# Where in a group of filling products the attention values are placed: two numbers in the rules that deal filling out

## The chip, the core and the metric

The kernel runs on one core of one Trainium2 chip. The metric is the device time of one execution in microseconds (us), as the median of several runs. A core has a matrix engine (PE, with weight loads shown as PEld), a vector engine (DVE), a scalar engine (ACT), a general engine (POOL) and a queue engine (SP) that issues most DMAs. Each engine works through its own list in order; semaphores hold an instruction until what it needs is done. PE writes only to PSUM, which has eight banks, and DVE and ACT read the banks out.

## The reference

One layer over 1024 tokens of width 1024 is computed in f32. The part that matters here is the mixer at its start, and above all the chunked attention:

```python
hn = rmsnorm(h, norm_mix_g[i])
z = hn @ w_in[i]
u = z[..., :POOL_W]                              # 512 columns: pooling mixer
q, k, v = jnp.split(z[..., POOL_W:], 3, axis=-1) # 8 heads of 64
a = pool_mixer(u, pool_w[i], pool_b[i], pool_scale[i])
# chunks of 64 queries, each with its own chunk and 8 earlier ones
s = jnp.einsum('bqhd,bkhd->bhqk', qb, kb).astype(jnp.float32) * scale + bias
pr = jax.nn.softmax(s, axis=-1).astype(vb.dtype)
o = jnp.einsum('bhqk,bkhd->bqhd', pr, vb)
h = h + jnp.concatenate([a, o], axis=-1) @ w_out[i]
```

After it come a gated MLP with a causal convolution, a gated per-layer embedding and a last norm. The change does not touch them.

## The kernel before

Every f32 product is made of three matmuls of rounded parts: high by high, high by low, low by high (`mm3`, lines 117 to 119). A step in `split` makes the two parts, the high one on ACT (line 122) and the low one on DVE (line 123).

The attention stage goes through 28 units. A unit `u` is a pair of heads `c` and one tile of 128 queries (the first unit of each pair of heads takes two tiles), so seven units make a pair of heads. Unit `u` puts on PE, in this order:

1. the transposes of the probabilities of unit `u - 1` (line 406), which ACT and DVE then copy out of banks 2, 3, 6 and 7 as high and low parts (`probs_out`, lines 424 and 426);
2. the scores of unit `u` (line 383) in banks 4 to 7, on which DVE and ACT then do the softmax: the least value (lines 351 or 355), the exponential (line 363), the reciprocal (line 365) and the scaling (line 361 on DVE, line 359 on ACT);
3. filling: products of the projections still to come, which keep PE at work while the softmax of unit `u` runs;
4. if unit `u - 1` ended a pair of query tiles, its attention values (`values(u - 1)`, lines 448 and 449): the probabilities of 256 queries times `V`, for both heads, in one bank. ACT and DVE then add the two halves of the result into `o32` (lines 451 and 454).

The filling is one long generator. It goes through 24 groups; a group is eight products of three matmuls (512 columns each) into bank 0 or bank 1 in turn, and the four groups of the second half of `V` are made of matmuls of 256 columns. After the last product of a group, DVE copies it out (line 263 for queries and keys, line 556 for the pooling columns, lines 254 and 255 for `V`); queries and keys are then split (lines 292 to 296), and weights of later groups are split when their turn comes (lines 469 and 472). `at[0]` holds how far the open group has come: 0.68 for each product, so 5.44 is the end of a group (5.76 for a group of `V`).

The attention values are put into the bank of the group before the open one. So they have to wait until DVE has copied that group out, and the group after the open one has to wait until lines 451 and 454 have read the values out of its bank. Both distances depend on where in the open group the values stand.

How much filling a unit takes is set by `credit`: each unit adds `ROOM[u % 7]`, each product takes 1. In `values`, more products are taken, at 0.5 each, while the open group has come less far than a bound. ACT and DVE instructions are collected with a due time (`push`) and put out sorted by it (`flush`): each at the unit's end, so their order on ACT and DVE follows the step of the filling at which they came up.

After unit 28, what is left of the filling is done, while ACT and DVE split the output weights and the first half of the attention result (`out_weights`, `cat_o`); then the output projection starts.

Of the kernel before, what the change touches and what calls it, by code (L numbers as in the profile page):

```python
# [73 lines left out]
NU = len(UNITS)  # L74
# [8 lines left out]
def trunk(tc, xT, pT, vecs, w_qk0, w_in, w_v, bias, counts, pool_w, w_out, w_up, w_down,  # L83
# [4 lines left out]
    with tc.tile_pool(name="sb", bufs=1) as sb, \  # L88
# [179 lines left out]
        def push(t, *fns):  # L268

            for n, fn in enumerate(fns):  # L270
                pending.append((t + 0.8 * n, len(pending), fn))

        def flush():
            todo = sorted(pending, key=lambda p: p[:2])
            pending.clear()
            owed.clear()
            for _, _, fn in todo:
                fn()
# [21 lines left out]
        def run_later(n):  # L300
            for fn in later[:n]:
                fn()
            del later[:n]
# [30 lines left out]
        def load_bias(h):  # L334
            b = biasb[h % 3]
            sp.dma_start(b, bias[h])

            def turned():
                act.activation(b, b, AF.Copy, scale=-1.0)
                pool.memset(b[0:64, 576:640], BIG)  # L340
                pool.memset(b[64:128, 0:64], BIG)
            return turned

        def softmax(todo, valued):

            for i, (x, b, ps, S, s_) in enumerate(todo):
                z = 2 * i / len(todo)

                def least(b=b, ps=ps, S=S, s_=s_):
                    if len(ps.shape) == 3:  # L350
                        dve.tensor_tensor_reduce(  # L351
                            S.rearrange("p (a b) -> p a b", a=2), ps,
                            b.rearrange("p (a b) -> p a b", a=2), 1.0, BIG, ALU.add, ALU.min, s_[:, 0:1])
                    else:
                        dve.tensor_tensor_reduce(S, ps, b, 1.0, BIG, ALU.add, ALU.min, s_[:, 0:1])

                def scaled(x=x, S=S, s_=s_):
                    if x:
                        act.activation(S, S, AF.Copy, scale=s_[:, 2:3])
                    else:  # L360
                        dve.tensor_scalar(S, S, s_[:, 2:3], None, ALU.mult)  # L361
                push(1.0 + 0.8 * z, least)
                push(1.9 + 0.85 * z, lambda S=S, s_=s_: act.activation(  # L363
                    S, S, AF.Exp, bias=s_[:, 0:1], scale=-1.0, accum_out=s_[:, 1:2]))
                push(max(2.95 + 0.01 * z, 1.91 + 0.85 * z) if valued else 2.95 + 0.55 * z, lambda s_=s_: dve.reciprocal(s_[:, 2:3], s_[:, 1:2]))
                push(3.9 + 0.1 * z if x else 3.0 + (0.01 if valued else 0.55) * z, scaled)
# [26 lines left out]
        def probs_t(u):  # L393

            c, ts = UNITS[u]
            total = key_tiles(u)

            def place(x, m):
                n = 2 * m + x
                return (2, HD * n) if n < 8 else (6, 384 + HD * (n - 8))  # L400

            for x in range(2):
                for m in range(total):
                    bank, col = place(x, m)
                    for y in range(2):
                        pe.transpose(PS[:, bank + y, col:col + HD], Sb[x][halves[y], m * P:(m + 1) * P],  # L406
                                     ident[halves[y], halves[y]], tile_position=(HD * y, 0))
            todo, m = [], 0
            for t in ts:
                nk = min(t + 1, BANDT)  # L410
                i0 = max(0, t - 4) - (t // 2 * 2 - 4)
                for a, b in ((0, min(nk, 4)), (4, nk)):
                    if b > a:
                        bank, col = place(0, m + a)
                        todo.append((t % 2 * P, i0 + a, i0 + b, bank, PS[:, bank:bank + 2, col:col + 2 * HD * (b - a)]))
                m += nk
            return todo

        def probs_out(todo, valued):
            for q, a, b, bank, ps in todo:  # L420
                src = ps.rearrange("p a (n q) -> p n a q", q=HD)
                hi, lo = [pt[:, a:b, :, q:q + P].rearrange("p k x (a q) -> p (k x) a q", a=2) for pt in PT]
                far = bank > 3
                push(3.5 if far else 0.0, lambda hi=hi, src=src: act.activation(hi, src, AF.Copy))
                push((3.55 if valued else 4.4) if far else 2.5 if valued else 3.7,
                     lambda lo=lo, src=src, hi=hi: dve.tensor_tensor(lo, src, rv(hi), ALU.subtract))  # L426

        credit, turns, valued = 0.0, [], [False]

        def values(u):  # L430
            nonlocal credit
            c_, ts = UNITS[u]
            w = ts[-1] // 2
            if ts[-1] % 2 == 0:
                return
            while c_ >= 2 and len(v_ready) < 2 * w + 2 or u < NU - 1 and at[0] < 1.6:
                next(fill)
                credit -= 0.5
                now[0] += STEP
            flush()  # L440
            ks = list(range(max(0, 2 * w - 4), 2 * w + 2))
            bank = (bankn[0] + 1) % 2 if u < NU - 1 else 5
            Os = [PS[:, bank, 256 * j:256 * j + 256] for j in range(2)]
            for j in range(2):
                O = Os[j]
                for n_, k in enumerate(ks):
                    idx = k - (2 * w - 4)
                    pe.matmul(O, V[:, k, 2 * c_ + j], PT[0][:, idx, j], start=n_ == 0, stop=False)  # L448
                    pe.matmul(O, V[:, k, 2 * c_ + j], PT[1][:, idx, j], start=False, stop=n_ == len(ks) - 1)  # L449
            for j in range(2):  # L450
                act.activation(otmp[halves[j]], Os[j][halves[1 - j]], AF.Copy)  # L451
            for j in range(2):
                a = halves[j]
                dve.tensor_tensor(o32[a, c_, w * 256:(w + 1) * 256], Os[j][a], otmp[a], ALU.add)
# [3 lines left out]
        at = [0]  # L458
# [183 lines left out]
        qk_ready, v_ready = [], []  # L642
        fill = rest()

        def lay_due(u):

            for c, x, h in list(qk_ready):
                if u >= (c - 1) * PER + (0 if x else PER - 1 if h else 2):
                    qk_ready.remove((c, x, h))
                    push(max(4.8, now[0] + 0.4), *lay(c, x, h))  # L650
# [4 lines left out]
        def unit(u):  # L655

            nonlocal credit
            now[0] = 0.0
            if u < NU:
                c, ts = UNITS[u]  # L660
                for h in range(2 if ts[-1] > 3 else 1):
                    while not all((c, x, h) in laid for x in range(2)):
                        next(fill)
                        lay_due(u - 1)
                        flush()
            valued[0] = u > 0 and UNITS[u - 1][1][-1] % 2 == 1
            if u:
                probs_out(probs_t(u - 1), valued[0])
            if u < NU:
                softmax(scores(u), valued[0])  # L670
                if u % PER == PER - 1:
                    for h in (2 * c + 3, 2 * c + 4):
                        if h < N_HEADS:
                            push(3.0, lambda h=h: turns.append(load_bias(h)))
                lay_due(u)
                credit += ROOM[u % PER]
                now[0] = 1.25
                while credit >= 1:
                    now[0] += STEP
                    credit -= 1  # L680
                    if next(fill, True) is False:
                        break
                    lay_due(u)
            else:
                for _ in range(DRAIN):
                    now[0] += STEP
                    next(fill)
            flush()
            if u:
                values(u - 1)  # L690
            if turns and (u % PER == PER - 1 or u % PER == 1):
                turns.pop(0)()
            run_later(LATER)
# [4 lines left out]
        with tc.manual_schedule(engines={mybir.EngineType.Activation, mybir.EngineType.DVE}):  # L698
            for u in range(NU + 1):
                unit(u)  # L700
                if u == NU - PER + 2:
                    sp.dma_start(pw, pool_w)
# [750 lines left out]
```

## Time and profile before

| what | value |
| --- | --- |
| median of 3 runs | 1129.33 us (1129.02 to 1129.41) |
| profiled execution | 1130.02 us |
| its span, first to last instruction | 1128.3 us |
| mean granted PE clock | 0.998 |
| PE busy | 1115.4 us, 99% of the span |
| DVE busy | 855.7 us, 76% |
| ACT busy | 586.3 us, 52% |

The span is followed in microseconds from its start. The units of the attention stage lie between about 54 and 266 us. In a row of the timeline the first number is the start, the second the duration, then come engine, line, operation, tiles and shape; a bracket at the end gives how long the engine was idle before, and what ended that. Matmuls overlap: one of 512 columns is shown with about 0.39 us, though the next starts 0.23 us later. So a wait of PE is read from start to start, and an idle time in a bracket is what is left of it after the modelled end of the matmul before.

### The profile page before, as it was taken

To read this page: it belongs to the slowest core of one execution; us is meant where nothing else is said; L and a number is where in the kernel's file an instruction comes from. 1 tells how busy PE (TensorE), PEld (TensorE's weight loads), DVE (VectorE), ACT (ScalarE), POOL (GpSimd) and SP (SyncE) were. 2 spreads that over 40 slices of the span, in tenths; PEclk is the share of its full clock that TensorE was granted. 3 is DMA by queue.
4 is the path that set the end of the run, shared out by engine and by line. 5 is a ranking of instruction groups with operands and counts; after the bars stand their busy time and mean duration, and the time that the engine had idled before them with its cause. 6 is when DMAs were issued, how large, how long until landed. Compare 5 with 4: busy or idle time off the path is not lost.

```text
span 1128.3 us, 16160 instructions
## 1 busy us (share of the span) xinstructions
PE 1115.4 (99%) x5914; PEld 934.0 (83%) x5914; DVE 855.7 (76%) x1456; ACT 586.3 (52%) x1020; POOL 166.3 (15%) x212
## 2 busy tenths in 40 slices
PE   9999999999999999999999999999999999999997
PEld 7988898888888888888888887888888888888887
DVE  7566766677768879877787777787877889986845
ACT  8376766665664644444443444344444444674634
POOL 0011001077002200210112011201120112000000
PEclk9999999999999999999999999999999999999999
DMA  7111110113510353774668455665576556520003
GB/s 280 38 38 43 39 40 24 59 57 112 188 55 10 91 159 95 159 168 131 159 149 176 133 159 140 154 165 140 151 157 168 132 154 128 149 94 19 1 34 116
DMA packets 64880, 125.92 MB, mean 112 GB/s; under 512 B 7328, under 2 KB 8736, under 8 KB 64800
## 3 DMA queue, kind: packets, MB, share of 16 engines
q1 hardware_dynamic: 50688, 99.38, 27.1%
q0 software_dynamic: 13824, 25.17, 14.0%
q8 instruction: 46, 0.75, 0.3%
q14 instruction: 34, 0.28, 0.1%
q10 hardware_dynamic: 288, 0.33, 0.1%
HBM read 110.18 MB, written 14.68 MB: 111 GB/s over the span
## 4 chain that ended last, share of the span: by engine, by line
PE 94%; DVE 2%; issue 1%; ACT 1%; DMA 0%; SPq 0%; POOL 0%; POOLq 0%; DVEq 0%; ACTq 0%
PE PS L117 29%; PE PS L118 29%; PE PS L119 29%; PE PS L383 2%; PE PS L448 2%; PE PS L449 2%; PE PS L406 1%; DVE B L426 1%; DMA F<-in_xT 0%; DVE F L351 0%; PE PS L770 0%; ACT F L363 0%; ACT F L451 0%; DVE F L361 0%; DVE BQ L123 0%
## 5 line engine op out<-in xcount | busy, mean ns | idle before, releaser
L117 PE MATMUL PS<-R 128*128 128x512 f32 (+1 forms) x1104 | 424.7, 385 | 1.6 <-ACT F L929 0.8
L119 PE MATMUL PS<-R 128*128 128x512 f32 (+1 forms) x1104 | 421.5, 382 | 0.4 <-DVE R L123 0.4
L118 PE MATMUL PS<-R 128*128 128x512 f32 (+1 forms) x1104 | 421.6, 382 | 0.3 <-DVE R L228 0.3
L117 PEld LDWEIGHTS PS<-R 128*128 128x128 f32 x1104 | 207.5, 188 | 45.4 <-issue 2.4
L119 PEld LDWEIGHTS PS<-R 128*128 128x128 f32 x1104 | 207.5, 188 | 41.3 <-DVE R L123 0.8
L118 PEld LDWEIGHTS PS<-R 128*128 128x128 f32 x1104 | 207.6, 188 | 40.2 <-DVE R L228 1.6
L122 ACT ACTIVATE R<-F 128x512 fp32r<-128x512 f32 (+2 forms) x221 | 137.3, 636 | 168.6 <-PE PS L118 83.0
L123 DVE TENSOR_TENSOR R<-F,R 128x512 fp32r<-128x512 f32 (+2 forms) x221 | 154.1, 713 | 40.7 <-ACT R L122 40.1
L842 DVE TENSOR_TENSOR F<-F 128x512 f32<-128x512 f32 x88 | 61.6, 700 | 52.6 <-DMA F<-in_w_up 49.8
L1152 DVE TENSOR_TENSOR F<-F,PS 128x512 f32<-128x512 f32 x140 | 92.5, 682 | 6.1 <-PE PS L119 5.8
L122 ACT ACTIVATE BQ<-RW 128x512 fp32r<-128x512 f32 x90 | 52.6, 622 | 75.5 <-PE PS L118 71.6
L1095 POOL DMA_DIRECT2D RW<-Yd x56 | 49.5, 884 | 259.9 <-DMA RW<-Yd 198.7
L1095 POOL DMA_DIRECT2D RW<-in_w_down x40 | 36.3, 951 | 235.9 <-DMA RW<-in_w_down 194.5
L123 DVE TENSOR_TENSOR BQ<-RW,BQ 128x512 fp32r<-128x512 f32 x90 | 59.1, 685 | 2.1 <-PE PS L118 1.3
L118 PE MATMUL PS<-BQ 128*128 128x512 f32 x140 | 54.6, 390 | 0.1
L978 ACT ACTIVATE F<-F,vec 128x1024 f32<-128x1024 f32 (+1 forms) x25 | 28.6, 1143 | 50.2 <-DVE F L953 44.0
L119 PE MATMUL PS<-BQ 128*128 128x512 f32 x140 | 54.5, 389 | 0.0
L118 PE MATMUL PS<-R,BQ 128*128 128x512 f32 x140 | 54.5, 389 | 0.0
L119 PE MATMUL PS<-R,BQ 128*128 128x512 f32 x140 | 54.5, 389 | 0.0
L117 PE MATMUL PS<-R,BQ 128*128 128x512 f32 x140 | 54.5, 389 | 0.0
L117 PE MATMUL PS<-BQ 128*128 128x512 f32 x140 | 54.5, 389 | 0.0
L363 ACT ACTIVATE F<-F,small 128x640 f32<-128x640 f32 (+4 forms) x64 | 44.0, 689 | 16.4 <-DVE small L351 13.5
(181 smaller groups left out, 1708.6 us busy)
## 6 DMA issues: line engine op xcount, KB each, us to landing
F<-in_w_up SPq DMA_DIRECT2D x91, 256.0 KB, 3.9
RW<-Yd SPq DMA_DIRECT2D x60, 256.0 KB, 3.7
RW<-Yd POOLq DMA_DIRECT2D x56, 256.0 KB, 5.0
RW<-in_w_down SPq DMA_DIRECT2D x50, 256.0 KB, 2.9
RW<-in_w_down POOLq DMA_DIRECT2D x40, 256.0 KB, 6.0
Yd<-F SPq DMA_DIRECT2D x40, 256.0 KB, 3.5
F<-in_w_in SPq DMA_DIRECT2D x10, 512.0 KB, 3.4
F<-in_xT SPq DMA_DIRECT2D x16, 256.0 KB, 5.8
```

The lines of the kernel that those rows point to most:

```text
L117: pe.matmul(ps, ahi, bhi, start=first, stop=False, skip_group_check=more)
L118: pe.matmul(ps, ahi, blo, start=False, stop=False, skip_group_check=more)
L119: pe.matmul(ps, alo, bhi, start=False, stop=last, skip_group_check=more)
L122: both = (act.activation(hi, src, AF.Copy), dve.tensor_tensor(lo, src, rv(hi), ALU.subtract))
L123: dve.tensor_tensor(lo, src, rv(hi), ALU.subtract))
L363: push(1.9 + 0.85 * z, lambda S=S, s_=s_: act.activation(S, S, AF.Exp, bias=s_[:, 0:1], scale=-1.0, accum_out=s_[:, 1:2]))
L383: pe.matmul(PS[:, places[x][y], 0:wide], q[halves[x], t * P:(t + 1) * P], k[halves[x], ki + y * wide:ki + (y + 1) * wide], start=i == 0, s ...
L448: pe.matmul(O, V[:, k, 2 * c_ + j], PT[0][:, idx, j], start=n_ == 0, stop=False)
L842: return dve.tensor_tensor(rawu[to], rawu[a], rawu[b], op)
L978: act.activation(y, Gb[:, 2 + a:2 + b], AF.Identity, bias=vec[:, C_CB + fi:C_CB + fi + 1], scale=cw(2))
L1095: pool.dma_start(t, src, accum_op=ALU.add)
L1152: dve.tensor_tensor(t, t, PS[:, 4 + d], ALU.subtract if n in (1, 5) else ALU.add)
```

## The change

Two rules change. In `values` the bound up to which products are taken goes from 1.6 to 2.3, so the values never stand after fewer than four products (2.72) of an open group. In `unit` the dealing of filling stops with one more product to be had (credit at least 1, under 2) if values follow in this unit and the open group stands at its seventh product (4.76; 5.04 in a group of `V`).

```diff
@@ def values(u):
-            while c_ >= 2 and len(v_ready) < 2 * w + 2 or u < NU - 1 and at[0] < 1.6:
+            while c_ >= 2 and len(v_ready) < 2 * w + 2 or u < NU - 1 and at[0] < 2.3:
                 next(fill)
                 credit -= 0.5
                 now[0] += STEP
@@ def unit(u):
                 while credit >= 1:
+                    if valued[0] and credit < 2 and 4.7 < at[0] < 5.4:
+                        break
                     now[0] += STEP
                     credit -= 1
                     if next(fill, True) is False:
```

Because the credit carries over, nearly every unit is dealt another number of products. The place `at[0]` at which the values of a unit stand:

| values of unit | 0 | 2 | 4 | 6 | 7 | 9 | 11 | 13 | 14 | 16 | 18 | 20 | 21 | 23 | 25 | 27 |
| --- | --- | --- | --- | --- | --- | --- | --- | --- | --- | --- | --- | --- | --- | --- | --- | --- |
| before | 2.04 | 4.08 | 2.04 | 4.76 | 3.40 | 5.44 | 3.60 | 2.16 | 5.76 | 2.04 | 5.44 | 2.72 | 2.04 | 4.08 | 2.04 | 2.04 |
| after | 2.72 | 4.76 | 2.72 | 4.76 | 4.08 | 2.88 | 5.04 | 2.88 | 2.72 | 4.08 | 2.72 | 4.76 | 3.40 | 2.72 | 4.76 | 4.76 |

Fewer products than before come in units 2, 7, 16, 20 and 22 (one less each) and 25 (two less, five instead of seven), and six 256-column matmuls less in units 11, 12 and 14. Four products fewer are left after the attention, nine instead of thirteen.

The first place is on PE, after the values of unit 9, where unit 11 begins. Before:

```order
L449 MATMUL PS<-B,R 128x256
L406 MATMUL PS<-ident,F 128x64 [waits DVE_49]
L406 MATMUL PS<-ident,F 128x64 x9
L406 MATMUL PS<-ident,F 128x64 [waits Activation_49]
L406 MATMUL PS<-ident,F 128x64 x9
L383 MATMUL PS<-R 128x320 x12
L117 MATMUL PS<-R 128x256 [waits DVE_49,Activation_49]
```

After:

```order
L449 MATMUL PS<-B,R 128x256
L406 MATMUL PS<-ident,F 128x64 x10
L406 MATMUL PS<-ident,F 128x64 [waits Activation_49]
L406 MATMUL PS<-ident,F 128x64 x9
L383 MATMUL PS<-R 128x320 x12
L117 MATMUL PS<-B,R 128x256 [waits Activation_49]
```

The filling product behind the scores began a group before and waited for DVE to free its bank; now it goes on in an open group, and waits only for split weights.

The second place is on DVE in unit 10, ahead of the same values: reciprocals and scaling of unit 10 (lines 365 and 361), then the sum of the values (line 454). Before:

```order
L426 TENSOR_TENSOR B<-PS,B 128x8x128
L365 RECIPROCAL small<-small 128x1 x2
L361 TENSOR_SCALAR F<-F,small 128x640
L454 TENSOR_TENSOR F<-PS,F 64x256 x2
L351 ISA F,small<-PS,F 128x640
```

After:

```order
L426 TENSOR_TENSOR B<-PS,B 128x8x128
L365 RECIPROCAL small<-small 128x1 x2
L361 TENSOR_SCALAR F<-F,small 128x640
L469 TENSOR_TENSOR B<-F,B 128x512 x2
L263 TENSOR_TENSOR F<-PS,F 128x512
L454 TENSOR_TENSOR F<-PS,F 64x256 x2
```

The group of queries that ends in unit 10 is now copied out (line 263) ahead of the values, and the split of weights for `V` (line 469) stands ahead of that copy.

The third place is on DVE in unit 25, which has two products less. Before:

```order
L365 RECIPROCAL small<-small 128x1
L361 TENSOR_SCALAR F<-F,small 128x640
L365 RECIPROCAL small<-small 128x1
L556 TENSOR_TENSOR F<-PS,F 128x512
L426 TENSOR_TENSOR B<-PS,B 128x8x128
L426 TENSOR_TENSOR B<-PS,B 128x2x128
```

After:

```order
L365 RECIPROCAL small<-small 128x1
L361 TENSOR_SCALAR F<-F,small 128x640
L365 RECIPROCAL small<-small 128x1
L426 TENSOR_TENSOR B<-PS,B 128x8x128
L426 TENSOR_TENSOR B<-PS,B 128x2x128
L556 TENSOR_TENSOR F<-PS,F 128x512
```

The copy of the group (line 556) moved behind the low parts of the probabilities (line 426).

## The prediction

> **What bounds the kernel now.** I read the busy times of the attention stage first, to see how much there is to win, and then PE's timeline at each wait in that stage.
>
> ```profile
> 54.00:266.00 212.00, 209.40 (x1724) 178.97 (x1723) 141.63 (x356) 137.36 (x290) 47.62 (x73) 1.00 0.14 45
> ```
>
> The columns behind the length are the busy times of PE, PEld, DVE, ACT and POOL. PE is idle for 2.60 of 212 us, at a full clock (1.00); it bounds the stage, and only its waits can be won. An idle time understates a wait, as a wait beside an undisturbed place shows:
>
> ```profile
> 230.17 0.39 PE L119 MATMUL PS<-R,B 128*128 128x512 f32 x1
> 230.40 0.28 PE L448 MATMUL PS<-B,R 128*128 128x256 f32 x1
> 230.51 0.28 PE L449 MATMUL PS<-B,R 128*128 128x256 f32 x1
> ...
> 244.77 0.39 PE L119 MATMUL PS<-R 128*128 128x512 f32 x1
> 245.50 0.38 PE L448 MATMUL PS<-B,R 128*128 128x256 f32 x1 [0.34 <-DVE F L556]
> 245.72 0.28 PE L449 MATMUL PS<-B,R 128*128 128x256 f32 x1
> ```
>
> Undisturbed (values of unit 23), the values start 0.23 us after the last filling matmul, and their next matmul 0.11 to 0.12 later. Those of unit 25 start 0.73 after it and go on 0.22 later: 0.50 + 0.10 = 0.60 us lost, 0.26 more than the bracket. A product, three matmuls, takes 3 x 0.228 = 0.68 us. The other waits:
>
> ```profile
> 70.90 0.39 PE L119 MATMUL PS<-R,B 128*128 128x512 f32 x1
> 71.22 0.71 PE L406 MATMUL PS<-ident,F 64*128 64x64 f32 x16
> 71.74 1.12 PE L383 MATMUL PS<-R 64*128 64x320 f32 x12
> 72.80 0.50 PE L117 MATMUL PS<-R,B 128*128 128x512 f32 x1
> ...
> 90.72 0.39 PE L119 MATMUL PS<-R 128*128 128x512 f32 x1
> 91.18 0.39 PE L448 MATMUL PS<-B,R 128*128 128x256 f32 x1
> ...
> 128.79 1.13 PE L383 MATMUL PS<-R 64*128 64x320 f32 x12
> 130.05 0.35 PE L117 MATMUL PS<-R 128*128 128x256 f32 x1
> ...
> 141.94 0.39 PE L448 MATMUL PS<-B,R 128*128 128x256 f32 x1 [0.35 <-DVE R L255]
> ...
> 169.41 0.47 PE L117 MATMUL PS<-R 128*128 128x512 f32 x1 [0.56 <-DVE F L454]
> 174.06 0.52 PE L406 MATMUL PS<-ident,F 64*128 64x64 f32 x10 [0.29 <-DVE B L426]
> 179.86 0.36 PE L448 MATMUL PS<-B,R 128*128 128x256 f32 x1 [0.53 <-DVE F L263]
> 199.42 0.47 PE L117 MATMUL PS<-R,B 128*128 128x512 f32 x1
> ...
> 224.04 0.39 PE L119 MATMUL PS<-R 128*128 128x512 f32 x1
> 224.61 0.41 PE L406 MATMUL PS<-ident,F 64*128 64x64 f32 x6 [0.18 <-DVE B L426]
> ```
>
> They fall into three kinds. The first four rows are undisturbed: filling to transposes 0.32, scores to filling 1.06.
>
> *Values that wait for the copy of the group before* (lines 263, 255, 556): 0.35 at 91.18 (0.46 instead of 0.23, and 0.1 behind it), 0.35 + 0.26 = 0.61 at 141.94, 0.53 + 0.26 = 0.79 at 179.86, and the 0.60 above: 2.35 us. These are units 4, 11, 16 and 25; all but 11 stood at 2.04.
>
> *Filling that waits for the values to leave the bank* (line 454): 1.26 instead of 1.06 at 130.05 (0.20), 0.20 for the same pattern at 199.42, and 0.56 + 0.07 = 0.63 at 169.41 (the 0.07 by the transposes below): 1.03 us. These are the values at 5.44, 5.44 and 5.76.
>
> *Transposes that wait for line 426*: 0.57 instead of 0.32 at 224.61 (0.25, that is 0.07 over its bracket), so 0.29 + 0.07 = 0.36 at 174.06: 0.61 us. This kind the change doesn't aim at.
>
> Together 3.99 us. I add 0.2 for starts too short for a bracket (values of unit 13, transposes of unit 12), an estimate: 4.2 us is the most that this stage can give.
>
> **The change part by part.** No instruction of PE is added or removed, so work costs nothing; only waits move.
>
> *What goes.* With four products of the open group ahead of them (2.72 instead of 2.04), the values of unit 4 find the copy done: it now comes up one product earlier and so stands ahead of the last line 426 on DVE, of which only later matmuls of the values have need. Units 16 and 25 stand at 4.08 and 4.76, where no copy lies ahead of them in their unit; neither does one for unit 11. The three at the end of a group now have one to four products between them and the next group, 0.68 us each where 0.20 or 0.63 was missing. All 3.38 us of the first two kinds go, and the 0.2.
>
> *What comes*, by units that got fewer products or a longer DVE list:
>
> ```profile
> 119.78 0.94 DVE L426 TENSOR_TENSOR B<-PS,B 128x768 fp32r<-128x768 f32 x1
> 120.64 0.68 DVE L263 TENSOR_TENSOR F<-PS,F 128x512 f32<-128x512 f32 x1
> ...
> 121.02 0.46 PE L406 MATMUL PS<-ident,F 64*128 64x64 f32 x8
> ...
> 125.52 0.56 DVE L361 TENSOR_SCALAR F<-F,small 128x640 f32<-128x640 f32 x1
> 125.58 0.83 ACT L359 ACTIVATE F<-F,small 128x640 f32<-128x640 f32 x1 [0.28 <-DVE small L365]
> 126.14 0.28 PE L448 MATMUL PS<-B,R 128*128 128x256 f32 x1
> 129.96 1.14 ACT L472 ACTIVATE B<-F 128x512 fp32r<-128x512 f32 x2
> 131.44 1.29 DVE L469 TENSOR_TENSOR B<-F,B 128x512 fp32r<-128x512 f32 x2
> ...
> 223.62 0.94 DVE L426 TENSOR_TENSOR B<-PS,B 128x768 fp32r<-128x768 f32 x1
> ...
> 228.55 2.20 POOL L570 TENSOR_TENSOR F<-F 128x271 f32<-128x271 f32 x3 [23.19 <-DVE F L556]
> ...
> 236.92 0.67 DVE L556 TENSOR_TENSOR F<-PS,F 128x512 f32<-128x512 f32 x1
> 237.51 1.55 DVE L426 TENSOR_TENSOR B<-PS,B 128x1024 fp32r<-128x1024 f32 x2
> 239.09 0.40 PE L406 MATMUL PS<-ident,F 64*128 64x64 f32 x6
> 243.71 0.80 DVE L361 TENSOR_SCALAR F<-F,small 128x640 f32<-128x640 f32 x1
> ```
>
> Units 2 and 16 become what unit 23 was, five products behind the same transposes and scores, with the same DVE list: the transposes after them start 0.99 after line 426 starts (223.62 to 224.61) and wait 0.25 each, 0.50 for both. Unit 23 itself gets six products and pays nothing.
>
> Unit 9 keeps six products, but the copy (0.59 to the next start, as 236.92 to 237.51) now stands ahead of line 426: 119.78 + 0.59 + 0.99 = 121.36 against 121.02, 0.34. DVE may start this unit up to 0.2 earlier, since unit 8 has a product more to clear its backlog; I take 0.25.
>
> Unit 25 has two products less: PE reaches its transposes at 239.09 - 1.37 = 237.72. Line 426 moves ahead of the copy, to 236.92; the first of its two takes about 1.2 of the 1.55, so they start near 238.2, and at the latest at 238.5: 0.48, at most 0.8.
>
> Unit 10 is the dearest. It did five products; now it does four and then 24 matmuls of 256 columns at 0.12, so PE would reach the values at 126.14 - 0.68 + 2.9 = 128.35. They now wait for the copy, which DVE gets to behind two splits, which stand behind two on ACT behind the scaling there: 125.58 + 0.83 = 126.41, first ACT split to 126.95, DVE splits to 128.25, copy to 128.9. That is 0.5 and 0.1 behind it: 0.6.
>
> Unit 15 has the copies of `V` (line 255) close ahead of its values: between nothing and the 0.61 of 141.94; 0.2, since its group ends four products ahead of the values.
>
> Sum of what comes: 0.50 + 0.25 + 0.48 + 0.60 + 0.20 = 2.03 us.
>
> The stop at the seventh product acts twice only, in units 7 and 21 (credit 1.5 and 1.0). Unit 7 has four products left; its values' bank has long been free, so nothing is late there.
>
> *The end of the stage.* Four products fewer, 2.73 us, cover the output weights.
>
> ```profile
> 260.22 0.64 ACT L472 ACTIVATE R<-F 128x512 fp32r<-128x512 f32 x1 [2.11 <-PE PS L118]
> 264.51 0.63 ACT L122 ACTIVATE R<-F 128x512 fp32r<-128x512 f32 x1 [3.65 <-DMA F<-in_w_out]
> 265.16 0.40 PE L117 MATMUL PS<-R,B 128*128 128x512 f32 x1
> 268.15 6.34 DVE L123 TENSOR_TENSOR R<-F,R 128x512 fp32r<-128x512 f32 x6
> ```
>
> Thirteen products from 265.16 end at 274.0, and the fourth product behind them needs the last split (274.49) at 276.1: 1.6 us spare. With nine it needs it at 273.4, and would be 1.1 late if the splits stayed. They don't: the split at 260.22 waited for the end of a group that now ends four products earlier in the unit, and the DMA of 264.51 waits for that split's buffer. The chain comes forward by about 1.5 us, and SP's order is unchanged. I cost it at nothing, 1.1 us if that cover is gone.
>
> *The sum.* What goes is the first two kinds, 3.38, the 0.61 of the third (units 16 and 23 as they were) and the 0.2: 4.19 us. What comes is 2.03. Net 2.16 us. Of the profiled 1130.02 us (span 1128.3 and 1.7 around it) 1127.9 are left; the median lies 0.69 below the profiled run, so 1129.33 - 2.16 = 1127.2 us.
>
> **The rivals.** 0.2% of this kernel, 2.26 us, is about what a measurement can tell from no change.
>
> *The new waits are hidden* (chance 0.14): unit 10's copy and unit 15's cost nothing, because ACT runs further ahead than in the rows. For it: DVE idles for a third of the stage (141.63 of 212). The net is 4.19 - 1.23 = 3.0 us, 3.4 if unit 25's transposes are on time too; 1126.1 us.
>
> *What goes comes back* (0.08): other units whose list got longer pay as unit 10 does; with three more such waits at 0.6 the net is 0.3, and the time 1129.0.
>
> *POOL in the way* (0.05): POOL's pooling sums begin a unit earlier and now lie over units 24 and 25, where the two missing products leave no room. The scaling at 243.71, with POOL at work, took 0.80 us where the one at 125.52 took 0.56. If the scaling of unit 25 waits for a whole POOL addition (2.20 / 3 = 0.73) instead of 0.24, its transposes wait 0.7 longer: net 1.5, 1127.9 us. The Trainium skill speaks for this: "SBUF — State Buffer", section "Who interferes with whom", has DVE instructions in a two-port mode, or with two inputs in SBUF, and POOL instructions block each other for a whole instruction. The trace agrees that a scaling is slowed, but by a third of an addition.
>
> *Slower* (0.06): DVE's chain in each unit, not PE, is what sets the unit's length wherever products are taken out. Ten products' worth were taken out of nine units (2, 7, 11, 12, 14, 16, 20, 22, and 25 twice); if each came back whole as 0.68 us of waiting, 6.8 us come for 4.2 that go, and the time is 1131.9. It decides from the point where over six of the ten come back. Against it: the 70 us of DVE's idle time, most of them in units with values, where DVE is through its list (125.52 + 0.56 in unit 10) before PE gets to the values (126.14).
>
> That the change does nothing can be ruled out: nearly all values stand elsewhere.
>
> **How the numbers follow.** The forecast has 0.67: net 2.16, down to 1.3 (unit 25 at 0.8, unit 9 at 0.34, unit 15 at 0.6) and up to 2.9 (units 10 and 15 near nothing). The bound of 2.26 cuts it in the middle: 0.34 of it counts as faster, 0.33 as the same. With the hidden waits faster has 0.48; with what comes back and POOL the same has 0.46; slower keeps 0.06. For eight times in ten the range goes from 1125.8 (net 3.5) to 1129.0 (net 0.3).
>
> **What would show it.** Right: PE's idle time between 54 and 266 us falls from 2.60 to about 1.2; no wait of filling for line 454 over 0.1, no wait of values for line 263 or 556 but in unit 10; transposes wait for line 426 in units 3, 17 and 26. Wrong: waits of values for line 426 or for lines 424 and 359 in units with five products or fewer, waits for line 123 at the start of the output projection, or an idle time that stays at 2.6.

## The result, and the profile after

The changed kernel takes 1127.92 us (median; the kernel before in the same comparison 1129.05 us), a ratio of 0.9987 with a 95% interval from 0.9981 to 0.9993. It is faster: by 1.1 us between the medians, and by 0.8 to 2.1 us by the interval. That is less than the 0.2% (2.26 us) that the prediction set as a bound, and the 1.1 us are about half of the 2.16 us that it worked out.

PE's waits in the stage, in the view that groups them (what waited, for what, us in total, times, longest), of the changed kernel:

```profile
PE PS L406 <- DVE B L426: 0.7, 3, 0.4
PE PS L448 <- DVE F L263: 0.5, 1, 0.5
PE PS L448 <- DVE R L255: 0.5, 1, 0.5
```

All waits for lines 454 and 556 are gone from this view. It has one wait of values each for lines 263 and 255, as before, but at new places: units 10 and 15 instead of 16 and 11. The row of the stage's busy times (PE's is the first):

```profile
54.00:263.00 209.00, 207.18 (x1702) 176.87 (x1701) 141.96 (x355) 135.90 (x288) 49.02 (x74) 1.00 0.13 43
```

PE is idle for 1.82 us instead of 2.60; 1.2 was forecast. PE's timeline of the changed kernel, at the waits that are new, in order of time:

```profile
70.33 0.39 PE L119 MATMUL PS<-R,B 128*128 128x512 f32 x1
70.88 0.71 PE L406 MATMUL PS<-ident,F 64*128 64x64 f32 x16 [0.16 <-DVE B L426]
...
120.74 0.39 PE L119 MATMUL PS<-R,B 128*128 128x512 f32 x1
121.23 0.71 PE L406 MATMUL PS<-ident,F 64*128 64x64 f32 x16
...
128.41 0.28 PE L119 MATMUL PS<-R 128*128 128x256 f32 x1
129.21 0.36 PE L448 MATMUL PS<-B,R 128*128 128x256 f32 x1 [0.52 <-DVE F L263]
...
168.29 0.39 PE L119 MATMUL PS<-R 128*128 128x512 f32 x1
169.14 0.39 PE L448 MATMUL PS<-B,R 128*128 128x256 f32 x1 [0.46 <-DVE R L255]
169.36 0.28 PE L449 MATMUL PS<-B,R 128*128 128x256 f32 x1
...
174.88 0.39 PE L119 MATMUL PS<-R 128*128 128x512 f32 x1
175.45 0.65 PE L406 MATMUL PS<-ident,F 64*128 64x64 f32 x14 [0.18 <-DVE B L426]
...
239.79 0.39 PE L119 MATMUL PS<-R 128*128 128x512 f32 x1
240.57 0.60 PE L406 MATMUL PS<-ident,F 64*128 64x64 f32 x10 [0.39 <-DVE B L426]
```

Read from start to start, against 0.32 for undisturbed transposes: 0.23 behind unit 2, 0.17 behind unit 9, 0.25 behind unit 16, 0.46 behind unit 25 (and 0.08 inside those transposes). The values in unit 10 start 0.80 after the last filling matmul. A short matmul is followed after 0.12, so that is 0.68, and 0.07 behind it: 0.75. Those in unit 15 start 0.85 instead of 0.23 after the last filling matmul, and their next matmul follows 0.22 instead of 0.12 later: 0.72 to 0.73.

A span mixes the stage with what lies around it. So I measure the stage by itself: from the first transposes of unit 1 to the first product after the last values, brought to nine products left (0.6825 us is added for each product beyond nine). Both ends, first of the kernel before (its second end, 265.16, stands in the prediction), then of the changed kernel:

```profile
59.27 0.40 PE L406 MATMUL PS<-ident,F 64*128 64x64 f32 x6
```

```profile
58.68 0.40 PE L406 MATMUL PS<-ident,F 64*128 64x64 f32 x6
...
266.14 0.40 PE L117 MATMUL PS<-R,B 128*128 128x512 f32 x1
```

Before: 265.16 - 59.27 + 4 x 0.6825 = 208.62 us. After: 266.14 - 58.68 = 207.46 us. The stage gained 1.16 us, which is what the medians gained (1.13). The rest of the 3.1 us by which the two profiled spans differ lies ahead of and behind the stage.

### The profile page after: what moved, and what is told of

Same layout as the page of the kernel before. It is cut to its first block, busy times and chain, and to the rows that moved or that the text cites. A ratio compares the mean times of both kernels' runs of the same rounds, so it can differ in the third digit from the quotient of the medians.

```text
span 1125.2 us, 16163 instructions
## 1 busy us (share of the span) xinstructions
PE 1114.5 (99%) x5914; PEld 934.1 (83%) x5914; DVE 856.0 (76%) x1456; ACT 585.2 (52%) x1020; POOL 164.9 (15%) x212
## 4 chain that ended last, share of the span: by engine, by line
PE 93%; DVE 3%; issue 1%; DMA 1%; ACT 1%; SPq 0%; POOL 0%; POOLq 0%; DVEq 0%; ACTq 0%
PE PS L117 29%; PE PS L118 28%; PE PS L119 28%; PE PS L383 2%; PE PS L448 2%; PE PS L406 2%; PE PS L449 2%; DMA F<-in_w_up 1%; DVE B L426 1%; DMA F<-in_xT 0%; PE PS L772 0%; DVE F L351 0%; ACT F L363 0%; DVE BQ L123 0%; ACT F L451 0%
```

## The experiments

Theory 1: every wait of PE is local; it has its price where it stands, and the gain is the sum. Theory 2: DVE and ACT have a fixed amount to do in a unit, so a wait that is removed comes back elsewhere. Theory 3: the gain lies outside the stage. All kernels together, with the stage measured as above:

| kernel | stage, us | against before | median, us | ratio to before (95%) |
| --- | --- | --- | --- | --- |
| before | 208.62 | | 1129.05 | |
| before, second profile | 208.60 | -0.02 | | |
| changed | 207.46 | -1.16 | 1127.92 | 0.9987 (0.9981 to 0.9993) |
| bound alone (rule1) | 208.78 | +0.16 | 1129.30 | 1.0001 (0.9992 to 1.001) |
| stop alone (rule2) | 208.11 | -0.51 | 1128.80 | 0.9995 (0.9986 to 1.0003) |
| changed, two orders (order2) | 206.23 | -2.39 | 1126.63 | 0.9978 (0.9969 to 0.9988) |
| changed, dealing (deal) | 206.38 | -2.24 | 1127.21 | 0.9981 (0.9972 to 0.9990) |
| both (all3) | 204.97 | -3.65 | 1125.55 | 0.9967 (0.9955 to 0.9978) |
| both and two more (all5) | 204.46 | -4.16 | 1125.12 | 0.9969 (0.9957 to 0.9981) |

The kernel before had medians of 1129.05, 1129.04 and 1129.13 us in the three comparisons (changed; rule1 to deal; all3 and all5). What the stage gained and what the medians gained agree within 0.5 us in every row.

**Is it the stage at all?** The kernel before, unchanged, profiled again.

> The kernel before, unchanged, profiled a second time, for the stretches on which the change has no instruction moved. Theory 1: from the first transposes of unit 1 to the last values it takes what the first profile showed within 0.1 us (211.35 less 2.73 for the four products more that are left), while the stretch before and the stretch behind differ by some tenths to 1.5 us from run to run. Theory 3 (the gain comes from outside the stage): the outer stretches repeat within 0.2 us, so that the 1.35 us by which the changed kernel's end was shorter is a difference of the kernels.

(The working in that text has a slip: the first profile's figure is 205.89 plus 2.73, which is the same 208.62.) The ends of the stage in the second profile of before:

```profile
59.00 0.40 PE L406 MATMUL PS<-ident,F 64*128 64x64 f32 x6
...
264.87 0.40 PE L117 MATMUL PS<-R,B 128*128 128x512 f32 x1
```

264.87 - 59.00 + 2.73 = 208.60 us: the stage repeats within 0.02 us. Its whole span was 1126.6 us instead of 1128.3, so the stretches outside moved by 1.7 us with nothing changed. Two waits of PE far behind the stage, between 600 and 900 us, make up 1.2 of them: 0.8 us for ACT (line 929) and 0.4 us for DVE (line 123) in the first profile, none in the second. The changed kernel's profile happens to lack them too. So theory 3 has no footing: the 1.9 us that its span lost outside the stage is about what two runs of one kernel differ by, and the medians gained what the stage gained.

**The two rules apart.** First the bound alone:

```diff
-            while c_ >= 2 and len(v_ready) < 2 * w + 2 or u < NU - 1 and at[0] < 1.6:
+            while c_ >= 2 and len(v_ready) < 2 * w + 2 or u < NU - 1 and at[0] < 2.3:
```

> The higher bound alone (2.3), without the stop at the seventh product. Theory 1 (each wait of PE is local and the gain is the sum of the waits): of the changed kernel's places only two become worse, the values of units 6 and 20 stand at 5.44 again, and the filling behind them waits 0.20 us each for line 454; unit 22 has five products instead of six and its transposes wait 0.25 for line 426. That is 0.65 us more waiting than in the changed kernel, a ratio to the kernel before near 0.9993 where the changed kernel has 0.9987. Theory 2 (the waits are set by what DVE and ACT have to do in a unit, and a wait that is removed comes back at another place): the waits of the attention stage add up to the changed kernel's, about 3.0 us, at other places, ratio 0.9987. Theory 3 (the gain lies outside the stage, by the four products fewer behind it): the same nine products are left at its end, so 0.9987 as well, whatever the waits.

It gained nothing; the stage is 1.32 us longer than the changed kernel's, where theory 1 had 0.65. Theory 1's third term, 0.25 behind unit 22, didn't come: those transposes start 0.32 after filling, undisturbed. PE at the start of unit 8, and DVE's line 454 there, in the kernel with the bound alone:

```profile
110.10 0.78 PE L383 MATMUL PS<-R 64*128 64x384 f32 x6
111.62 0.47 PE L117 MATMUL PS<-R,B 128*128 128x512 f32 x1 [0.74 <-ACT B L424]
...
216.85 0.47 PE L117 MATMUL PS<-R 128*128 128x512 f32 x1 [0.74 <-ACT B L424]
```

```profile
110.62 0.86 DVE L454 TENSOR_TENSOR F<-PS,F 64x256 f32<-64x256 f32 x2 [2.80 <-ACT F L451]
```

The bracket names line 424 on ACT, which filling doesn't need. What it needs by the program is its bank: line 454 reads the values out of it until 111.48, and PE goes on at 111.62. (Line 424 happens to end at 111.48 too, so the times alone don't tell the two apart.) The same stretch in the changed kernel:

```profile
108.69 0.77 PE L383 MATMUL PS<-R 64*128 64x384 f32 x6
109.39 0.50 PE L117 MATMUL PS<-R 128*128 128x512 f32 x1
...
109.96 0.40 PE L119 MATMUL PS<-R 128*128 128x512 f32 x1
110.21 0.47 PE L117 MATMUL PS<-R,B 128*128 128x512 f32 x1
110.52 0.40 PE L118 MATMUL PS<-R,B 128*128 128x512 f32 x1
```

From the scores to filling it is 1.52 instead of 0.70 us: the wait is 0.82 us in unit 8, and unit 22 (216.85) has the same, not 0.20 as behind unit 9. These two units are the second of a pair of heads: they have six score matmuls and twelve transposes, where unit 11 has twelve and twenty, so PE has less to do between the values and the filling. And 0.82 less one product (0.68) leaves 0.14: that is about the wait that the changed kernel still has there, at the second product (109.96 to 110.21 and 110.21 to 110.52 are 0.25 and 0.31 instead of 0.23 each, 0.10 together). So the rows give 2 x 0.82 - 2 x 0.14 = 1.36 us, where the stage has 1.32. On top of the bound, the stop, which acts in two units only, is worth more than the whole net gain.

Then the stop alone:

```diff
+                    if valued[0] and credit < 2 and 4.7 < at[0] < 5.4:
+                        break
```

> The stop at the seventh product alone, with the old bound of 1.6. The values of units 9, 14 and 18 move from 5.44, 5.76 and 5.44 to 4.76, 5.04 and 4.76; units 4, 11, 16 and 25 stay where they were before. Theory 1: the filling behind units 9, 14 and 18 loses its waits of 0.20, 0.63 and 0.20 us, the waits of values in units 4, 11, 16 and 25 stay (2.35 us together), and the transposes behind unit 16 lose 0.36, for that unit has six short matmuls more: 1.0 to 1.4 us gained, ratio 0.9988 to 0.9991. Theory 2: what goes there comes back, ratio 0.9998 to 1.0002. Theory 3: thirteen products stay at the end, as before, so nothing is gained, 1.000.

The waits for line 454 and the 0.36 behind unit 16 went, 1.39 us, as theory 1 had it, but two new ones came. PE behind units 11 and 15, with the stop alone:

```profile
134.74 0.28 PE L119 MATMUL PS<-B,R 128*128 128x256 f32 x1
135.28 0.28 PE L406 MATMUL PS<-ident,F 64*128 64x64 f32 x2 [0.27 <-DVE B L426]
...
166.61 0.28 PE L449 MATMUL PS<-B,R 128*128 128x256 f32 x1
167.25 0.34 PE L406 MATMUL PS<-ident,F 64*128 64x64 f32 x4 [0.37 <-DVE F L361]
```

Undisturbed it would be 0.21 in both places: 0.33 and 0.43, and with the 0.07 to 0.08 within the transposes 0.91 us together. 1.39 - 0.91 = 0.48; the stage gained 0.51, where theory 1 had 1.0 to 1.4. The expectation had not listed these two units; the sum over waits holds once they are in it. But it is no mere gap in a list: in both units DVE's rows start when they did in the kernel before (line 426 at 134.02 against 133.97, line 361 at 166.78 against 166.75), and PE, which comes earlier, waits for them. At these two places theory 2 is right: a wait that was removed came back.

**The two dear waits, by order alone.** PE's order stays; on DVE and ACT three entries are pushed with an earlier due time, two for the copy of V (lines 254 and 255) and one for the copy of the queries (line 263).

```diff
-                    push(now[0], hi)
-                    push(now[0] + 0.5, lo)
+                    push(now[0] - 1.0 * (t0 == 6), hi)
+                    push(now[0] + 0.5 - 1.0 * (t0 == 6), lo)
...
-                    push(now[0] if valued[0] else max(now[0], 3.6), lambda: qk_out(x, h, ps))
+                    push(now[0] - 0.5 * ((p, x, h) == (2, 0, 1)) if valued[0] else max(now[0], 3.6), lambda: qk_out(x, h, ps))
```

> The changed kernel, with PE's order untouched; on DVE the copy of the group that ends in unit 10 (line 263) goes ahead of the two weight splits (line 469), and on ACT the two readings of V that end in unit 15 (line 254) go ahead of the scaling (line 359). Theory 1: the waits of the values of units 9 and 14, 0.75 and 0.73 us in the changed kernel, fall under 0.1 each, and no other wait grows: 1.4 us less, ratio 0.9974 to 0.9976 where the changed kernel has 0.9987. Theory 2: DVE and ACT have as much to do as before, so the time comes back at the next places where PE needs them, the matmuls of V behind the split weights in unit 11 and the transposes of unit 16: ratio 0.9987. Theory 3: nothing changes at the ends of the stage, 0.9987.

The ACT and DVE rows in unit 15 of the changed kernel:

```profile
166.83 0.62 ACT L359 ACTIVATE F<-F,small 128x384 f32<-128x384 f32 x1 [1.14 <-DVE small L365]
167.36 0.82 ACT L254 ACTIVATE R<-PS,small 128x256 fp32r<-128x256 f32 x2
...
168.21 0.88 DVE L255 SCALAR_TENSOR_TENSOR R<-PS,small,R 128x256 fp32r<-128x256 f32 x2 [1.02 <-ACT R L254]
```

The same lines, and PE's in unit 15, with the two orders:

```profile
165.39 0.84 ACT L254 ACTIVATE R<-PS,small 128x256 fp32r<-128x256 f32 x2 [0.28 <-PE PS L119]
166.25 0.62 ACT L359 ACTIVATE F<-F,small 128x384 f32<-128x384 f32 x1
...
166.53 0.87 DVE L255 SCALAR_TENSOR_TENSOR R<-PS,small,R 128x256 fp32r<-128x256 f32 x2
...
167.71 0.39 PE L119 MATMUL PS<-R 128*128 128x512 f32 x1
167.94 0.28 PE L448 MATMUL PS<-B,R 128*128 128x256 f32 x1
```

In the changed kernel ACT stands idle for 1.14 us ahead of the scaling, and line 254 queues behind it; then DVE, idle for 1.02, ends line 255 at 169.09, and the values start at 169.14. With line 254 ahead of the scaling, in ACT's idle time, line 255 is done at 167.40, and the values start undisturbed, 0.23 after filling. In unit 10 likewise: they start at 128.69, 0.12 after a matmul of 256 columns. Both waits are gone, 1.48 us, and nothing came at the places that theory 2 named. The stage gained 1.23, not 1.4, since one wait grew, the transposes behind unit 25:

```profile
239.48 0.34 PE L406 MATMUL PS<-ident,F 64*128 64x64 f32 x4 [0.63 <-DVE B L426]
```

0.63 instead of 0.39 in the bracket. The cause is POOL, below.

**The transposes, by dealing.** One product is moved from the unit after to the unit that is short.

```diff
-                while credit >= 1:
+                while credit >= 1 - (u in (2, 16, 25)):
```

> The changed kernel, with one product more in each of units 2, 16 and 25 and one less in units 3, 17 and 26, which have values between their filling and the next transposes; all values stand where the changed kernel has them. Theory 1: the transposes behind units 2, 16 and 25 lose their waits for line 426, 0.23, 0.25 and 0.55 us, and those behind units 3, 17 and 26 have the values as cover (0.8 to 2.75 us) and pay nothing: 1.0 us less, ratio 0.9978 where the changed kernel has 0.9987. Theory 2: the product taken away in units 3, 17 and 26 comes back as a wait there, ratio 0.9987. Theory 3: 0.9987.

PE behind unit 25 with this dealing:

```profile
240.08 0.39 PE L119 MATMUL PS<-R 128*128 128x512 f32 x1
240.40 0.78 PE L406 MATMUL PS<-ident,F 64*128 64x64 f32 x18
```

0.32, undisturbed; so it is behind units 2 and 16, and only the 0.17 behind unit 9 is left of the waits for line 426. 1.08 us gained where 1.03 was expected. The product taken out of units 3, 17 and 26 cost nothing: the values cover it.

**Together, and the rest.** The two edits together:

> The changed kernel with both earlier edits together: the two orders on DVE and ACT in units 10 and 15, and one product more in units 2, 16 and 25. Theory 1 (waits are local and add up): from the first transposes of unit 1 to the last values the changed kernel took 207.46 us, the orders alone took 1.23 off that and the dealing alone 1.08; together 2.3, so about 205.1 us, and a time of 0.9967 to 0.9971 of the kernel before. The transposes behind unit 25, which waited 0.78 us with the orders alone, have 0.68 more ahead of them and wait 0.1 at most. Theory 2 (waits come back): the two gains overlap, 206 us or more, ratio 0.9978 or above.

The stage takes 204.97 us; the ratio is 0.9967. The gains add up: 2.51 us by the waits (1.48 and 1.03), 2.49 measured, since the 0.23 behind unit 25 is gone too. Then the last three waits, with two more edits:

```diff
-                    if valued[0] and credit < 2 and 4.7 < at[0] < 5.4:
+                    if valued[0] and (credit < 2 and 4.7 < at[0] < 5.4 or u in (7, 21) and 4 < at[0] < 5):
...
-                    push(now[0] - 0.5 * ((p, x, h) == (2, 0, 1)) if valued[0] else max(now[0], 3.6), lambda: qk_out(x, h, ps))
+                    push(now[0] - 0.5 * ((p, x, h) == (2, 0, 1)) if valued[0] else max(now[0], 3.6) + ((p, x, h) == (2, 0, 0)), lambda: qk_out(x, h, ps))
```

> The kernel of all3, and two more edits for the waits that it should still have: dealing stops one product earlier in units 7 and 21 (the values of units 6 and 20 then stand at 4.08 and two products of the open group lie behind them, not one), and the copy of the group that ends in unit 9 (line 263) goes behind line 426 on DVE. Theory 1: the filling in units 8 and 22 loses 0.13 us each, the transposes behind unit 9 lose 0.17; 0.4 us less than all3, about 204.7 us from the first transposes to the last values, ratio 0.9964 to 0.9967, and no wait of PE over 0.1 us in the stage. Theory 2: as all3, or longer, since the values of unit 9 or the split of unit 9's copy come late instead.

The busy times of this last kernel from 59 to 264 us, by stretches (PE's is the first), and below it the same stretch of the kernel before:

```profile
59.00:264.00 205.00, 205.00 (x1702) 176.64 (x1701) 139.89 (x341) 134.11 (x279) 51.37 (x77) 1.00 0.15 46
```

```profile
59.00:264.00 205.00, 202.40 (x1679) 172.99 (x1678) 138.15 (x340) 133.12 (x277) 45.78 (x70) 1.00 0.14 45
```

PE is idle for 0.00 of 205 us. The stage is 4.16 us shorter than before, against the 4.2 us that the prediction gave as the most that this stage can give. By time it can't be told from all3 (1125.12 and 1125.55 us), and its ratio, 0.9969, isn't below all3's 0.9967, though 0.9964 to 0.9967 was expected. Both are faster than the kernel before, and by all that is on record than the changed kernel: the changed kernel's interval begins at 0.9981, where that of all5 ends, and above that of all3. The ratios of order2 and deal, 0.9978 and 0.9981, are 0.0002 to 0.0004 above what was expected, well inside their intervals.

**POOL.** The changed kernel without POOL's sums.

> The changed kernel without POOL's pooling sums for three of the four column groups (lines 570 and 580 to 584 are left out on POOL, so the pooled columns are wrong). If POOL's instructions hold DVE's scaling up: the scalings of units 24 to 27 (line 361) take 0.56 us each instead of 0.72 to 1.03, line 426 of unit 25 comes 0.16 us earlier, and the transposes behind unit 25 wait 0.39 us instead of 0.55. If the scalings are long for another reason: they stay at 0.7 to 1.0 and the wait stays at 0.55. What lies outside the stage may move too, since POOL's work there is left out; only the stage is read.

Half a miss. DVE in unit 25 without POOL's sums, and PE's transposes there:

```profile
238.50 0.55 DVE L361 TENSOR_SCALAR F<-F,small 128x640 f32<-128x640 f32 x1
239.12 0.16 DVE L365 RECIPROCAL small<-small 128x1 f32<-128x1 f32 x1
...
239.69 0.39 PE L119 MATMUL PS<-R 128*128 128x512 f32 x1
240.46 0.34 PE L406 MATMUL PS<-ident,F 64*128 64x64 f32 x4 [0.39 <-DVE B L426]
```

All four scalings from unit 24 on took 0.55 to 0.56, so it is POOL that makes them long. But the wait stayed at 0.39 in the bracket: behind the scaling DVE has the second reciprocal, which needs ACT's sum of the second exponential, read out until 239.09, and line 426 stands behind that. In the changed kernel the longer scaling (0.72) hides under that; with the two orders (0.95) it doesn't: ACT's sum is read out at 237.87 there, but the reciprocal starts at 238.16, behind the scaling, and the transposes pay the 0.23. That is read from the rows of that run; the two orders without POOL's sums were not run.

## Why the prediction was right, and where it was off

The time, 1127.92 us, lies within the range and 0.7 us above the forecast of 1127.2. Part of that closeness is luck: the forecast started from the 1129.33 us of three runs, and the kernel before has 1129.05 over 22. The net gain, 1.16 us in the stage, is 1.0 less than the 2.16 worked out, and just below the 1.3 to 2.9 that the main forecast allowed. The mechanism, waits that go at known places and waits that come at others, was right; one wait that comes was much too small in the sum. Step by step:

- *What goes*: as forecast. In the changed kernel all waits of the first two kinds are gone at the units named, and so is the one behind unit 23; behind unit 16, 0.25 of the 0.36 is there again, as the prediction had it among what comes. By the measured stage gain of 1.16 and the waits that came (below, 2.82), what went was 3.98 us; the prediction had 4.19, with 0.2 of it an estimate.
- *What comes, transposes*: 0.23, 0.25, 0.17 and 0.55 us, where 0.25, 0.25, 0.25 and 0.48 were forecast. The sum is 1.20 against 1.23.
- *What comes, unit 10*: 0.75 us, where 0.60 was forecast. The place in the queue was right: on DVE's timeline (the row below, in unit 10 of the changed kernel) the copy ends at 129.06, worked out was 128.9. PE was ready at 128.53 (worked out: 128.35). What I had left out is the 0.15 from the end of the copy to the matmul (129.21).

```profile
128.38 0.68 DVE L263 TENSOR_TENSOR F<-PS,F 128x512 f32<-128x512 f32 x1
```

- *What comes, unit 15*: **this step was mis-sized.** 0.20 was taken, "between nothing and the 0.61 of 141.94", because the group ends four products ahead. It is 0.73, above the upper end. I had priced it by a distance on PE, and not by the queue of ACT and DVE as in unit 10. On ACT the scaling (line 359) stands ahead of line 254 and waits for a reciprocal (line 365), which on DVE stands behind a weight split and line 426. The experiment with the two orders shows that this queue is the whole of it.
- *Filling in unit 22*: costed at nothing, because there are "0.68 us each where 0.20 or 0.63 was missing". In units 8 and 22, 0.82 is missing, as the bound alone showed; one product leaves about 0.14 in each (0.10 of it shows in the starts). In unit 8 that wait stood in the kernel before as well (110.89 to 111.20, 0.31 instead of 0.23), so only the one in unit 22 came. So "no wait of filling for line 454 over 0.1" was at its limit.
- Sum of what comes: 1.20 + 0.75 + 0.73 + 0.14 = 2.82 us measured, 2.03 forecast. Unit 15 has 0.53 of the difference of 0.79, unit 10 0.15, unit 22 0.14, and the transposes are 0.03 below. With unit 8's old wait the changed kernel's waits add up to about 2.95 us, and its stage is 3.00 longer than that of the last kernel, where PE is never idle: so no wait of any size is missing from the list.
- *The end of the stage*: costed at nothing, and right, but not for the reason given. The view of PE's waits shows none in the output projection's start, and PE runs on from 266.14 with no idle time. The chain was to come forward by 1.5 us. ACT's split at 260.22 did (it ends at 259.40 instead of 260.86), but the one that waits for the DMA behind it starts at 264.46, as before (264.51). The last DVE split is nevertheless done at 273.34 instead of 274.49: the last four took 3.03 us together, where six took 6.34 before. POOL's sums, begun earlier, end at 270.98 in the changed kernel and run past 276 in the kernel before, and without POOL's sums four such splits take 2.50 us. So POOL, which the prediction had only as a rival, helped here.

Of the rivals, the hidden waits fell on both counts (0.75 and 0.73). What goes comes back is refuted as the general mechanism: in order2, deal and all3 removed waits stayed removed, but for the 0.23 behind unit 25. It held at two places of the stop alone (units 11 and 15, 0.91 us). The slower case, a unit's length set by DVE's chain, falls with the last kernel, where PE has no idle time though DVE's work in that stretch is no less (139.89 against 138.15 us). POOL's place was right (unit 25) and its price in the changed kernel 0.01 us (0.78 from filling to transposes, 0.77 without POOL's sums).

## What to carry to other kernels

When an engine at 99% waits at a dozen known places, price each by the list of every engine that it waits for, at its own unit; a distance on the waiting engine, or the price of a like place elsewhere, was off by a factor of about four in two places here. A wait for a copy at the end of a queue can be removed by moving that entry forward in the queue, with the waiting engine's work left as it is: three due times gave 1.2 us here. To compare effects of 0.1%, cut the stretch in question out of the profile: in two profiles of one kernel it repeated within 0.02 us, where the span moved by 1.7.

## What the runs showed of the hardware

A DVE scaling that is held up by a POOL addition or subtraction isn't slowed in proportion to the overlap; it ends a fixed time after POOL's instruction does. Three pairs, POOL's row first, with the two orders:

```profile
235.83 2.06 POOL L570 TENSOR_TENSOR F<-F 128x271 f32<-128x271 f32 x3
...
237.28 0.95 DVE L361 TENSOR_SCALAR F<-F,small 128x640 f32<-128x640 f32 x1
```

In the changed kernel:

```profile
236.91 2.06 POOL L570 TENSOR_TENSOR F<-F 128x271 f32<-128x271 f32 x3
...
238.60 0.72 DVE L361 TENSOR_SCALAR F<-F,small 128x640 f32<-128x640 f32 x1
```

In the kernel before (its scaling, 243.71 with 0.80, stands in the prediction):

```profile
243.43 0.73 POOL L584 TENSOR_TENSOR F<-F 128x248 f32<-128x248 f32 x1
```

POOL's instructions end at 237.89, 238.97 and 244.16, the scalings at 238.23, 239.32 and 244.51: 0.34, 0.35 and 0.35 us later, however much they overlap. Without POOL's sums a scaling takes 0.55. So the scaling is held until POOL's instruction is done. It also goes the other way. In unit 24 with the two orders:

```profile
228.12 0.55 DVE L361 TENSOR_SCALAR F<-F,small 128x640 f32<-128x640 f32 x1
228.17 1.00 POOL L570 TENSOR_TENSOR F<-F 128x271 f32<-128x271 f32 x1
```

Here the scaling isn't held, and POOL's addition takes 1.00 us instead of 0.63 or 0.64. In the changed kernel the same two start at 229.44 and 229.49, again 0.05 us apart, and there the scaling is held (1.03 us): starts this close don't tell which of the two will wait.

The prediction read the 0.24 us of one row as a slowing by a third of an addition; it was the rest of that instruction. The Trainium skill, "SBUF — State Buffer", section "Who interferes with whom", says that whichever of POOL and a DVE instruction in a two-port mode is issued first keeps the shared ports for its whole instruction. These traces agree that one waits for the whole of the other; the longest scaling in them takes 1.03 us, 0.48 more than alone. That the 0.2 us by which 0.35 falls short of 0.55 is the scaling's start-up, done while it is held, would fit. So would a scaling of the kernel before that starts at 252.38: a POOL addition ends 0.13 us later, and it takes 0.55. But no run here takes it apart.
